# Fixed places for the fourth and fifth norm in a hybrid encoder block: sums and row spreads between value and query products, and the second quarter's query and key products pass by pass

## The chip, the cores and the metric

The kernel runs on one core of one Trainium2 chip. The metric is device time in microseconds of a whole execution, as the median of several executions: 1527.71 us before the change (three runs, 1527.10 to 1528.05). Beside it stands one execution recorded by the hardware profiler, which names every instruction of every engine with its start and its length. PE is the matrix engine (TensorE), DVE the vector engine (VectorE), ACT the scalar engine (ScalarE), POOL is GpSimd, and SP (SyncE) issues most of the data transfers (DMAs).

## The reference, cut to what matters

One block of an encoder on 1024 frames and 16 learned meta tokens, 1024 features wide: a norm, a token mixer with four mLSTM heads and four retention heads, a second norm, and a gated MLP with a causal convolution.

```
def rmsnorm(x, g):
    y = xf * lax.rsqrt(jnp.mean(xf * xf, axis=-1, keepdims=True) + EPS)
    return (y * g)
...
    h = jnp.concatenate([meta, x], axis=1)
    h = h + token_mixer(rmsnorm(h, norm_mix_g[l]), w_in[l], ...)
    h = h + channel_mixer(rmsnorm(h, norm_ffn_g[l]), ...)
    return rmsnorm(h, norm_final_g)[:, N_META:]
```

Inside the token mixer `proj = up @ w_in` gives queries, keys, values and gates of all heads. The change lies at the very beginning: the first norm, and the first products of its result with the weights of head 4.

## The kernel before, in words

**Layout.** Features lie on the 128 partitions and positions on the free axis. Each product of 32-bit numbers is made of three products of a rounded type: high part times high part, high times low, low times high. So every operand is split in two: ACT copies it to the rounded type (the high part), and DVE subtracts that from the original (the low part). The normed stream is held in four blocks named after the half of the positions and the half of the features: "11" and "12" (first half of the positions), "21" and "22" (second half). `UB[...]` holds high and low part, `u21h` and `u21l` in the profile. Later, sums and differences of the blocks (S1 to S4) are made too, for a Winograd-like scheme with seven products in place of eight; `usum` and `usplit` make them.

**The five norms.** The 1040 positions are normed in five ranges (`RNG`): 144, 128 and 256 positions of the first half, 272 and 256 of the second. Counted from one, the fourth norm is `r = 3` and the fifth `r = 4`. One norm has these steps:

- `norm_sums` (L850): ACT squares both feature halves (L855, L863), DVE adds them (L867) and halves the sum again (L870, remembered as `last["added"]`); PE then sums over the partitions (L826, "pca"), ACT takes the root (L828) and DVE the reciprocal (L829, "rcola"). With `late=True` the part from the PE sums on is returned as a function, to be called later.
- `norm_rows`: PE spreads the reciprocal over the partitions (L838, "pra").
- `norm_split` (L882): DVE scales with the gain and the spread factor, eight instructions (L890); ACT casts each feature half to the high part (L891); DVE subtracts the low parts (L895, `last["pace"]`).

**The products around them.** `v4_group(c, ...)` makes values and gate inputs of head 4 for one chunk of 128 positions, with the stream as the stationary operand: three passes (high-high, high-low, low-high) of eight matmuls each (L954). ACT evacuates the values (L957) and DVE the gate inputs (L958). `q4_group(i, half, j0, j1, ...)` makes queries (i = 0) or keys (i = 1) of head 4 for one quarter of the positions, 24 matmuls, the three products of one feature block right behind each other (L901 to L903), and an evacuation by ACT (L966, "rawq", "rawk"). `q4_pair` makes queries and keys of the first quarter together and pass by pass: high-high for both, then high-low, then low-high (L979), with the third norm's sums ahead of the first pass and its row spread ahead of the second.

**What sets the order.** Up to the products of the output gate of head 4 ("o" products, po4x and po4y, L911 to L913), nothing is fixed but data dependencies and the pairs that `after(later, first)` adds: the framework's scheduler simulates the engines' time and takes, for each engine, what it holds to be ready, earlier written work first. So matmuls that are written later fill places that it thinks would stand empty: in the profile of before, query products stand between those of a value group. From the o products on (`pinned[0] = True`) PE, DVE and ACT follow program order, which a planner inside the kernel has dealt out with costs of its own. Transfers are not pinned. Each engine's queue is then executed in order.

**The stretch of the change** (L1782 to L1850): norm 1, value group 1 with norm 2, groups 0 and 2, the pair of the first quarter with norm 3, norm 4's sums, groups 3 and 4, norm 4's split, norm 5's sums, queries and keys of the second quarter, norm 5's split, the sums of blocks for S1 and S2, groups 5 and 6, queries and keys of the third quarter, groups 7 and 8, queries and keys of the last quarter, the split of S3, two copies of block "12" into other buffers (x12, L1845), and the split of S4. The products go round a ring of PSUM banks (pa, pb, sA, num). The buffers of S3 are those of block 21's parts, those of S1 are the raw blocks 11 and 22; the rotation tables (`tables_load`, "A<-rot_d" in the profile) are loaded into the buffers that S1's sums leave.

Of the kernel before, what the change touches and what calls it, by code (L numbers as in the profile page):

```python
# [36 lines left out]
SB = 528  # L37
# [52 lines left out]
def body(ctx, tc, h_in, vecs, cst, mask_in, rot, w_v0, w_vp, w_g, w_out, w_up, w_gate, w_down, out):  # L90
# [10 lines left out]
    def dep(later, first, sync):  # L101
        kind = mybir.DependencyClass.Sync if sync else mybir.DependencyClass.NoSync
        tc.add_manual_dep(later.ins, first.ins.name, mybir.DependencyInfo(kind, mybir.DependencyReason.DATA), reason="order")

    def after(later, first):
        dep(later, first, False)

    last = {}
    G, PE, V, AC = nc.gpsimd, nc.tensor, nc.vector, nc.scalar
# [114 lines left out]
    raws = [st.tile([P, T], F32, name=f"raw{x}") for x in "qk"]  # L224
# [60 lines left out]
    def pp(name, tag):  # L285
        return ps.tile([P, 512], F32, tag=tag, name=name, bufs=PSB[tag])
# [94 lines left out]
    def spawn(g, q=pend, key=None):  # L381
        if dealt[0]:
            if next(g, pend) is not pend:
                q.append(g)
                until[id(g)] = fin[0]
                owner[id(g)] = key
        else:
            for _ in g:
                pass
# [262 lines left out]
    sums = {(g, st_, k): dram.tile([P, 2 * HB], F32, name=f"ws{g}{st_}_{k}") for g, n in (("w", 8), ("d", KD)) for st_ in ("65", "73") for k in range(n)}  # L652
# [166 lines left out]
    def rms_sums(ss, t0, t1, nm, col, tag, more=()):  # L819
        n = t1 - t0  # L820
        o = n % P
        subs = ([(0, P, o)] if o else []) + [(i, P, P) for i in range(o, n, P)]
        pc = rps("pc" + nm, tag)
        for i, (o, w, _) in enumerate(subs):
            for a in (ss, *more):
                last["sums"] = PE.matmul(pc[:w, i:i + 1], a[:, o:o + w], cs[:, C_M01 + P - 1:C_M01 + P], start=a is ss, stop=a is (ss, *more)[-1])  # L826
        ns = len(subs)
        last["sqrt"] = AC.activation(col[:, :ns], pc[:, :ns], AF.Sqrt, bias=epsc, scale=1.0 / D)  # L828
        last["recip"] = V.reciprocal(col[:, :ns], col[:, :ns])  # L829
        return n, subs, pc, col, nm  # L830
# [19 lines left out]
    def norm_sums(r, late=False):  # L850
        half, j0, j1 = RNG[r]
        n = j1 - j0
        xs = [xf[f"{half + 1}{i + 1}"][:, :, j0:j1] for i in (0, 1)]
        sq = [x[:, :, j0:j1] for x in sqs]
        m = AC.activation(sq[0], xs[0], AF.Square)  # L855
        if r:
            after(m, last["sqrt"])
        if r < 2:
            m = V.tensor_tensor(sq[1], xs[1], xs[1], ALU.mult)
            if r:  # L860
                after(m, last["scale"])
        else:
            after(AC.activation(sq[1], xs[1], AF.Square), last["sqrt"])  # L863
        if r == 1:
            ss = [x[:, k] for x in sq for k in range(4)]
        else:
            m = V.tensor_tensor(sq[0], sq[0], sq[1], ALU.add)  # L867
            if r:
                after(m, last["pace"] if r in (2, 3) else last["recip"])
            last["added"] = V.tensor_tensor(sq[0][:, 0:2], sq[0][:, 0:2], sq[0][:, 2:4], ALU.add)  # L870
            ss = [sq[0][:, k] for k in range(2)]

        def sums():
            norms[r] = xs, rms_sums(ss[0], 0, n, f"a{r}", tmp.tile([P, 5], F32, tag="rcol", name=f"rcola{r}"), "tr", ss[1:])
        if late:
            return sums
        sums()

    def norm_rows(r):
        norms[r] += (rms_rows(norms[r][1], None, "upd"),)  # L880

    def norm_split(r):  # L882
        half, j0, j1 = RNG[r]
        if len(norms[r]) < 3:
            norm_rows(r)
        xs, got, pr = norms.pop(r)
        parts_ = [[u[:, :, j0:j1] for u in UB[f"{half + 1}{i + 1}"]] for i in range(2)]
        for i, x in enumerate(xs):
            for k in range(4):
                last["scale"] = V.scalar_tensor_tensor(x[:, k], x[:, k], vec[:, V_MIX + 4 * i + k:V_MIX + 4 * i + k + 1], pr, ALU.mult, ALU.mult)  # L890
            m = last["cast"] = AC.copy(parts_[i][0], x)  # L891
            if r == 0:
                last["first"] = m
        for x, (h_, l_) in zip(xs, parts_):
            last["pace"] = V.tensor_tensor(l_, x, h_.bitcast(F32), ALU.subtract)  # L895
        if r == 0:
            for i, x in enumerate(xs):
                V.tensor_copy(ug[:, 4 * i:4 * i + 4], x[:, :, :32])
# [31 lines left out]

    vtile[4] = [vslot(0, "v4lo"), vslot(1, "v4hi")]

    def v4_group(c, tag, between=None):
        t0, L = CH[c]
        nv = 264
        pv = pp(f"pv4_{c}", tag)
        if c == 0:
            for i in range(2):
                for j in range(4):
                    after(PE.matmul(pv[32 * j:32 * j + 32, :nv], ug[:, 4 * i + j, :], w0raw[i][:, j * nv:(j + 1) * nv],  # L940
                                    start=i == 0, stop=i == 1, tile_position=(0, 32 * j)), last["rows"])
            t = vz[:META, 264:264 + nv]
            spawn(quads(t, pv, nv))
            V.tensor_copy(gts[:META, :, 0, :], t[:, DV:].rearrange("p (a b) -> p a b", a=2))
            return
        half = c > 4
        j0 = t0 - 512 * half
        for i, j in ((0, 0), (0, 1), (1, 0)):
            if i and between:
                between()  # L950
            for kb in range(KB):
                u = UB[f"{half + 1}{kb // 4 + 1}"][i]
                o = kb % 4 * nv
                m = PE.matmul(pv[:, :nv], u[:, kb % 4, j0:j0 + L], (w0hi, w0lo)[j][kb // 4][:, o:o + nv], start=i + j + kb == 0, stop=i == 1 and kb == KB - 1, skip_group_check=True)  # L954
                if i and between:
                    after(m, last["rows"])
        AC.copy(vtile[4][half][:, (c - 1) % 4 * VW:(c - 1) % 4 * VW + DV], pv[:, :DV])  # L957
        V.tensor_copy(gts[:, :, c, :], pv[:, DV:nv].rearrange("p (a b) -> p a b", a=2))  # L958

    def q4_group(i, half, j0, j1, tag):  # L960
        w = need(("q4", i), 1 - i)
        pt = pp(f"pq4{i}{half}{j0}", tag)[:, :j1 - j0]
        for kb in range(KB):
            u = UB[f"{half + 1}{kb // 4 + 1}"]
            mm3(pt, tuple(x[:, kb % 4 * P:(kb % 4 + 1) * P] for x in w[kb // 4]), tuple(x[:, kb % 4, j0:j1] for x in u), kb == 0, kb == KB - 1)
        AC.copy(raws[i][:, half * 512 + j0:half * 512 + j1], pt)  # L966

    def q4_pair(half, j0, j1, tags, between):
        w = [need(("q4", i), 1 - i) for i in range(2)]
        pt = [pp(f"pq4{i}{half}{j0}", tags[i])[:, :j1 - j0] for i in range(2)]  # L970
        for p, (a, b) in enumerate(((0, 0), (0, 1), (1, 0))):
            if p == 0:
                between()
            if p == 1:
                norm_rows(2)
            for i in range(2):
                for kb in range(KB):
                    u = UB[f"{half + 1}{kb // 4 + 1}"][b]
                    m = PE.matmul(pt[i], w[i][kb // 4][a][:, kb % 4 * P:(kb % 4 + 1) * P], u[:, kb % 4, j0:j1], start=p + kb == 0, stop=p == 2 and kb == KB - 1, skip_group_check=True)  # L979
                    after(m, last["rows" if p else "sums"])  # L980
        AC.copy(raws[0][:, half * 512 + j0:half * 512 + j1], pt[0])
        yield
        after(AC.copy(raws[1][:, half * 512 + j0:half * 512 + j1], pt[1]), last["cast"])

    ROWS = [("x", "11"), ("y", "12"), ("x", "S2"), ("y", "S1"), ("x", "S3"), ("y", "S4"), ("x", "22")]
# [794 lines left out]
    ring0 = tag_ring()  # L1780
# [10 lines left out]
    v4_group(2, next(ring0))  # L1791
    third = norm_sums(2, True)
    need(("q4", 0), 1)
    pair = q4_pair(0, 0, 272, [next(ring0), next(ring0)], third)
    next(pair)
    norm_split(2)
    next(pair, None)
    norm_sums(3)
    for c in (3, 4):
        v4_group(c, next(ring0))  # L1800
    norm_split(3)
    norm_sums(4)
    for i in range(2):
        q4_group(i, 0, 272, SB, next(ring0))
    norm_split(4)

    s1 = [st.tile([P, 2 * SB], F32, tag=f"A{i + 1}", name=f"s1_{i}").rearrange("p (k j) -> p k j", k=2) for i in range(2)]
# [1 line left out]
    def part(x, i):  # L1809
        return s1[i] if x == "S1" else xf[x][:, 2 * i:2 * i + 2]  # L1810
# [19 lines left out]
    usum(1, "11", "12", "12")  # L1830
    usplit("S1", "S1", "uh3", "ul3")
    need(("o", 4, 1), 0)
    for c in (5, 6):
        v4_group(c, next(ring0))
    for i in range(2):
        q4_group(i, 1, 16, 272, next(ring0))
    for c in (7, 8):
# [4 lines left out]
    x12 = [vslot(2 + i, f"s4_{i}").rearrange("p (k j) -> p k j", k=2) for i in range(2)]  # L1842
    tables_load(4)
    for i in range(2):
        AC.copy(x12[i], part("12", i))  # L1845
    s1[:] = x12
    need(("o", 4, 1))
    usplit("S4", "S1", "uh2", "ul2")
# [719 lines left out]
```

## Time and profile before

| | us |
|---|---|
| median of three runs | 1527.71 (1527.10 to 1528.05) |
| the profiled execution | 1526.2 |
| its span, first to last instruction | 1524.4 |
| PE busy in the span | 1486.6 |
| DVE busy | 1090.0 |
| ACT busy | 756.4 |
| POOL busy | 72.1 |
| mean granted PE clock | 0.996 of full |

A line of the profile in order of time reads: start, length, engine, line of the kernel, operation, output<-inputs, tile shape, types, how many instructions are merged, and in brackets the idle time before them with what ended it. Times are microseconds from the first instruction. A matmul's length is that of its passage through a pipeline, so products that follow each other start every 0.12 us though each is shown with 0.28. In the list of waits the three numbers are the total, how often, and the longest.

### The profile page before, as it was taken

The page shows a single profiled execution, that of the slowest core. Times are in us where ns is not written, and L with a number is a line of the kernel's source. Part 1 is how long each engine was busy: PE and PEld are TensorE (multiplying, and loading weights), DVE is VectorE, ACT ScalarE, POOL GpSimd, SP SyncE. Part 2 cuts the span into 40 slices and gives each one's busy share as a digit, 9 for nine tenths or more (in the row PEclk, how much of TensorE's full clock was granted, in tenths as well). Part 3 has the DMA queues.
Part 4 walks back from the last instruction along what each step waited for, and adds up shares of the span by engine and source line. Part 5 has one row for each costly group of instructions (what it writes and reads, how often), then busy time and mean ns, then how long its engine had stood idle before and what let it go on. Part 6 is the DMA issues. An engine that isn't in the chain of part 4 may idle for free.

```text
span 1524.4 us, 25487 instructions
## 1 busy us (share of the span) xinstructions
PE 1486.6 (98%) x9929; PEld 1348.3 (88%) x9929; DVE 1090.0 (72%) x2087; ACT 756.4 (50%) x1455; POOL 72.1 (5%) x157
## 2 busy tenths in 40 slices
PE   7989999999999999999999999999999999999997
PEld 7888999999999999987888998999999999888887
DVE  6785868678777677846867787767666666778667
ACT  4465655554655455554454565444444444344443
POOL 1000000000000000000000001222220000000000
PEclk9999999999999999999999999999999999999999
DMA  6022255323533355697333248887772224933313
GB/s 232 2 87 60 84 161 195 110 78 118 186 120 98 125 166 185 198 394 262 110 114 132 80 128 239 199 210 191 178 196 78 83 81 157 370 105 109 97 42 111
DMA packets 104586, 223.81 MB, mean 147 GB/s; under 512 B 10520, under 2 KB 33760, under 8 KB 104288
## 3 DMA queue, kind: packets, MB, share of 16 engines
q1 hardware_dynamic: 89824, 191.68, 37.8%
q0 software_dynamic: 8448, 23.07, 7.6%
q10 hardware_dynamic: 6192, 7.41, 1.4%
q8 instruction: 78, 1.28, 0.3%
q14 instruction: 44, 0.36, 0.1%
HBM read 178.05 MB, written 67.15 MB: 161 GB/s over the span
## 4 chain that ended last, share of the span: by engine, by line
PE 88%; DVE 7%; DMA 3%; ACT 1%; issue 1%; DVEq 0%; SPq 0%; ACTq 0%
PE pdx L913 3%; PE pdx L912 3%; PE pdx L911 3%; PE pup_x L912 2%; PE pga_x L911 2%; PE pup_x L913 2%; PE pup_x L911 2%; PE pga_x L912 2%; PE pga_x L913 2%; PE pdy L913 2%; PE pdy L912 2%; PE pdy L911 2%; PE n L1603 2%; PE pwx L913 2%; PE u L1601 2%; PE pwx L911 2%
## 5 line engine op out<-in xcount | busy, mean ns | idle before, releaser
L782 ACT CAST hi_up<-raw_up 128x512 fp32r<-128x512 f32 (+1 forms) x52 | 36.4, 719 | 107.7 <-PE pga_z L912 61.1
L783 DVE TENSOR_TENSOR lo_up<-raw_up,hi_up 128x512 fp32r<-128x512 f32 (+1 forms) x52 | 41.3, 810 | 38.2 <-ACT hi_up L782 37.5
L783 DVE TENSOR_TENSOR lo_ga<-fraw_ga,hi_ga 128x512 fp32r<-128x512 f32 (+1 forms) x52 | 41.9, 809 | 37.1 <-ACT hi_ga L782 36.9
L911 PE MATMUL pup_x<-uh_g,hi_up 128*128 128x256 f32 (+1 forms) x240 | 67.2, 283 | 1.2 <-ACT uh_g L1965 1.2
L912 PE MATMUL pup_x<-ul_g,hi_up 128*128 128x256 f32 (+1 forms) x240 | 67.4, 282 | 0.1
L913 PE MATMUL pup_x<-uh_g,lo_up 128*128 128x256 f32 (+1 forms) x240 | 66.4, 282 | 0.0
L783 DVE TENSOR_TENSOR lo_d<-rd,hi_d 128x1024 fp32r<-128x1024 f32 (+1 forms) x34 | 37.7, 1114 | 32.8 <-ACT hi_d L782 32.7
L782 ACT CAST hi_ga<-fraw_ga 128x512 fp32r<-128x512 f32 (+1 forms) x52 | 36.4, 719 | 45.4 <-PE pup_z L912 21.9
L913 PE MATMUL pdx<-uh_d,lo_d 128*128 128x512 f32 (+1 forms) x156 | 57.9, 375 | 0.0
L912 PE MATMUL pdx<-ul_d,hi_d 128*128 128x512 f32 (+1 forms) x156 | 57.8, 374 | 0.0
L782 ACT CAST hi_d<-rd 128x1024 fp32r<-128x1024 f32 (+1 forms) x34 | 32.3, 959 | 49.2 <-PE pdy L912 32.5
L913 PE MATMUL pdy<-uh_d,lo_d 128*128 128x512 f32 x132 | 51.9, 393 | 0.0
L912 PE MATMUL pdy<-ul_d,hi_d 128*128 128x512 f32 x132 | 51.7, 392 | 0.0
L911 PE MATMUL pdx<-uh_d,hi_d 128*128 128x512 f32 (+1 forms) x156 | 48.5, 372 | 0.0
L911 PE MATMUL pdy<-uh_d,hi_d 128*128 128x512 f32 x132 | 47.9, 389 | 0.0
L911 PE MATMUL pga_x<-uh_g,hi_ga 128*128 128x512 f32 x120 | 47.5, 396 | 0.0
L912 PE MATMUL pga_x<-ul_g,hi_ga 128*128 128x512 f32 x120 | 47.5, 396 | 0.0
L911 PEld LDWEIGHTS pup_x<-uh_g,hi_up 128*128 128x128 f32 x240 | 45.3, 189 | 2.3 <-ACT uh_g L1965 1.4
L913 PE MATMUL pga_x<-uh_g,lo_ga 128*128 128x512 f32 x120 | 47.1, 393 | 0.0
L912 PEld LDWEIGHTS pup_x<-ul_g,hi_up 128*128 128x128 f32 x240 | 45.4, 189 | 1.0 <-DVE ul_g L1966 0.3
L913 PEld LDWEIGHTS pup_x<-uh_g,lo_up 128*128 128x128 f32 x240 | 44.8, 189 | 0.8
L1670 DVE SCALAR_TENSOR_TENSOR mx<-tr,vec,sig 128x386 f32<-128x386 f32 (+2 forms) x42 | 24.0, 571 | 21.5 <-PE tr L1662 16.0
(1698 smaller groups left out, 5738.8 us busy)
## 6 DMA issues: line engine op xcount, KB each, us to landing
raw_up<-w_up_d SPq DMA_DIRECT2D x22, 512.0 KB, 6.4
fraw_ga<-w_gate_d SPq DMA_DIRECT2D x22, 512.0 KB, 5.0
acts<-cv SPq DMA_DIRECT2D x44, 256.0 KB, 4.2
wsd<-w_down_d POOLq DMA_DIRECT2D x44, 256.0 KB, 7.0
rd<-wsd SPq DMA_DIRECT2D x22, 512.0 KB, 3.6
raw_w<-w_out_d SPq DMA_DIRECT2D x20, 512.0 KB, 6.8
wsw<-raw_w SPq DMA_DIRECT2D x32, 256.0 KB, 3.2
raw_m<-w_out_d SPq DMA_DIRECT2D x14, 512.0 KB, 4.0
```

The lines of the kernel that those rows point to most:

```text
L782: AC.copy(hi[:, o:o + n], x)
L783: V.tensor_tensor(lo[:, o:o + n], x, hi[:, o:o + n].bitcast(F32), ALU.subtract)
L911: m.append(PE.matmul(pt, ah, xh_, start=first and k == 0, stop=False, skip_group_check=True))
L912: PE.matmul(pt, ah, xl_, start=False, stop=False, skip_group_check=True)
L913: m.append(PE.matmul(pt, al, xh_, start=False, stop=last and k == n - 1, skip_group_check=True))
L1601: PE.matmul(up[:, :nv], kw[:L], v, start=True, stop=True)
L1603: PE.matmul(pn[:L, :nv], pt[:L, :L], v, start=True, stop=c == 0)
L1670: return V.scalar_tensor_tensor(dst, tr[:, x0 - t0:x1 - t0], vec[:, g:g + 1], sig(b, p)[:, x0 - a0:x1 - a0], ALU.mult, ALU.mult)
```

## The change

- Norm 4's sums on PE are called inside a `q4_pair` for the second quarter, which takes the place of its two `q4_group` calls; its row spread comes between the queries' and the keys' high-high products. Queries of that pass are ordered after the sums, all later products of the pair after the rows. Both evacuations of this pair are ordered after the last cast of norm 4.
- `norm_split` is divided into `norm_scale` (scaling and casts) and `norm_lows` (low parts). Between the two of norm 4 stand norm 5's squares and their sum on DVE, ordered after norm 4's scaling (before: after the last reciprocal); norm 4's low parts are ordered after that sum.
- Value groups 5 and 6 move ahead of norm 5's split. Norm 5's sums on PE stand ahead of group 5's low-high pass, and its row spread ahead of group 6's high-low pass, with the products around them ordered after them.
- The two x12 copies are ordered after the last raw copy (`last["raw"]`).

```diff
             if r:
-                after(m, last["pace"] if r in (2, 3) else last["recip"])
+                after(m, last["pace"] if r in (2, 3) else last["scale"] if r == 4 else last["recip"])
...
+    def norm_split(r):
+        norm_scale(r)
+        norm_lows(r)
+
+    def norm_scale(r):
...
+    def norm_lows(r):
+        xs, parts_ = scaled.pop(r)
         for x, (h_, l_) in zip(xs, parts_):
             last["pace"] = V.tensor_tensor(l_, x, h_.bitcast(F32), ALU.subtract)
+            if r == 3:
+                after(last["pace"], last["added"])
...
-    def v4_group(c, tag, between=None):
+    def v4_group(c, tag, between=None, at=1):
...
         for i, j in ((0, 0), (0, 1), (1, 0)):
-            if i and between:
+            hooked = between and (i or j > at - 1 and not at)
+            if between and (i, j) == ((1, 0) if at else (0, 1)):
                 between()
...
-                if i and between:
+                if hooked:
                     after(m, last["rows"])
...
-        AC.copy(raws[i][:, half * 512 + j0:half * 512 + j1], pt)
+        last["raw"] = AC.copy(raws[i][:, half * 512 + j0:half * 512 + j1], pt)
...
-            if p == 1:
-                norm_rows(2)
+            if p == 1 and r == 2:
+                norm_rows(r)
             for i in range(2):
+                if r == 3 and p == 0 and i:
+                    norm_rows(r)
...
-                    after(m, last["rows" if p else "sums"])
-        AC.copy(raws[0][:, half * 512 + j0:half * 512 + j1], pt[0])
+                    after(m, last["rows" if p or r == 3 and i else "sums"])
+        if r == 2:
+            AC.copy(raws[0][:, half * 512 + j0:half * 512 + j1], pt[0])
         yield
+        if r == 3:
+            after(AC.copy(raws[0][:, half * 512 + j0:half * 512 + j1], pt[0]), last["cast"])
         after(AC.copy(raws[1][:, half * 512 + j0:half * 512 + j1], pt[1]), last["cast"])
...
-    norm_sums(3)
+    fourth = norm_sums(3, True)
     for c in (3, 4):
         v4_group(c, next(ring0))
-    norm_split(3)
-    norm_sums(4)
-    for i in range(2):
-        q4_group(i, 0, 272, SB, next(ring0))
+    pair = q4_pair(0, 272, SB, [next(ring0), next(ring0)], 3, fourth)
+    next(pair)
+    norm_scale(3)
+    fifth = norm_sums(4, True)
+    norm_lows(3)
+    next(pair, None)
+
+    def fifth_sums():
+        fifth()
+        last["rows"] = last["sums"]
+    v4_group(5, next(ring0), fifth_sums)
+    v4_group(6, next(ring0), lambda: norm_rows(4), 0)
     norm_split(4)
...
-    for c in (5, 6):
-        v4_group(c, next(ring0))
...
     for i in range(2):
-        AC.copy(x12[i], part("12", i))
+        after(AC.copy(x12[i], part("12", i)), last["raw"])
```

More of the change, by code (lines that the diff above doesn't have):

```diff
@@ L880, in norm_rows @@
         norms[r] += (rms_rows(norms[r][1], None, "upd"),)
+    scaled = {}
     def norm_split(r):
+        norm_scale(r)
+        norm_lows(r)
+    def norm_scale(r):
         half, j0, j1 = RNG[r]
@@ L887, in norm_split @@
         parts_ = [[u[:, :, j0:j1] for u in UB[f"{half + 1}{i + 1}"]] for i in range(2)]
+        scaled[r] = xs, parts_
         for i, x in enumerate(xs):
@@ L965, in q4_group, with q4_pair @@
             mm3(pt, tuple(x[:, kb % 4 * P:(kb % 4 + 1) * P] for x in w[kb // 4]), tuple(x[:, kb % 4, j0:j1] for x in u), kb == 0, kb == KB - 1)
-        AC.copy(raws[i][:, half * 512 + j0:half * 512 + j1], pt)
-    def q4_pair(half, j0, j1, tags, between):
+        last["raw"] = AC.copy(raws[i][:, half * 512 + j0:half * 512 + j1], pt)
+    def q4_pair(half, j0, j1, tags, r, between):
         w = [need(("q4", i), 1 - i) for i in range(2)]
@@ L1793, in body @@
     need(("q4", 0), 1)
-    pair = q4_pair(0, 0, 272, [next(ring0), next(ring0)], third)
+    pair = q4_pair(0, 0, 272, [next(ring0), next(ring0)], 2, third)
     next(pair)
```

## The prediction

> **What bounds the kernel now.** I read the page first, then busy time by stretch, then each engine in order of time, then the chain of work that ended last.
>
> ```profile
> span 1524.4 us, 25487 instructions
> PE 1486.6 (98%) x9929; PEld 1348.3 (88%) x9929; DVE 1090.0 (72%) x2087; ACT 756.4 (50%) x1455; POOL 72.1 (5%) x157
> ```
>
> TensorE (PE) carries the kernel, and a change in order can only win where PE stands still. Busy time by stretch (first the length, then busy us and count for PE, PEld, DVE, ACT, POOL, then granted clock, DMA share, GB/s):
>
> ```profile
> 33.00:46.70 13.70, 13.70 (x116) 13.50 (x114) 7.91 (x13) 4.46 (x9) 0.00 (x0) 1.00 0.01 2
> 46.70:73.00 26.30, 24.77 (x209) 24.77 (x209) 23.83 (x37) 10.89 (x18) 0.00 (x0) 1.00 0.01 2
> 73.00:93.00 20.00, 15.73 (x138) 14.57 (x136) 17.46 (x28) 15.96 (x27) 0.00 (x0) 1.00 0.48 159
> 93.00:126.00 33.00, 29.29 (x213) 27.25 (x214) 22.36 (x66) 15.34 (x33) 0.33 (x3) 0.95 0.26 66
> 126.00:160.00 34.00, 34.00 (x256) 32.62 (x254) 22.83 (x56) 20.59 (x40) 0.11 (x1) 1.00 0.07 24
> ```
>
> PE is idle 1.53 us before 73, 4.27 us from 73 to 93, 3.71 us from 93 to 126, and not at all for the next 34 us. So what the edited stretch (33 to 73) wins must pass the two loose stretches behind it; from 126 on PE is the bound and keeps what arrives. PE in order of time:
>
> ```profile
> 39.08 0.28 PE L902 MATMUL pq<-u11l,hi_q 128*128 128x256 f32 x1
> ...
> 40.29 1.39 PE L826 MATMUL pca<-cs,sqr 128*128 128x1 f32 x12
> ...
> 44.46 0.83 PE L838 MATMUL pra<-cs,rcola 128*128 128x16 f32 x6
> ...
> 48.23 1.24 PE L954 MATMUL pv<-w0hiq,u21h 128*128 128x264 f32 x8 [1.53 <-ACT u21h L891]
> ...
> 49.54 0.95 PE L826 MATMUL pca<-cs,sqr 128*128 128x1 f32 x8
> ...
> 56.21 0.61 PE L838 MATMUL pra<-cs,rcola 128*128 128x128 f32 x4
> ...
> 71.08 0.28 PE L903 MATMUL pq<-u21h,lo_q 128*128 128x256 f32 x1
> ...
> 72.62 0.28 PE L911 MATMUL po4x<-u11h,hi_o 128*128 128x258 f32 x1
> ...
> 76.18 0.39 PE L911 MATMUL po4x<-u11h,hi_o 128*128 128x256 f32 x1 [1.95 <-ACT rawk L966]
> ...
> 90.36 0.28 PE L913 MATMUL po4x<-uS3h,lo_o 128*128 128x256 f32 x1
> 92.95 0.39 PE L911 MATMUL po4y<-uS4h,hi_o 128*128 128x258 f32 x1 [2.31 <-ACT sig L1003]
> ```
>
> The fourth norm's sums end at 41.68 (40.29 + 1.39); its row spread (L838) comes 2.8 us later, behind query and key products that the scheduler put first. So u21h is late and PE runs out at 46.70. VectorE (DVE) over the same time:
>
> ```profile
> 37.11 0.73 DVE L870 TENSOR_TENSOR sqr<-sqr 128x544 f32<-128x544 f32 x1
> ...
> 42.01 0.18 DVE L829 RECIPROCAL rcola<-rcola 128x3 f32<-128x3 f32 x1 [2.16 <-ACT rcola L828]
> 43.91 1.22 DVE L867 TENSOR_TENSOR sqr<-sqr,sqr 128x1024 f32<-128x1024 f32 x1 [1.71 <-ACT sqr L863]
> 45.32 3.36 DVE L890 SCALAR_TENSOR_TENSOR x<-x,vec,pra 128x272 f32<-128x272 f32 x8 [0.19 <-PE pra L838]
> 48.59 0.69 DVE L870 TENSOR_TENSOR sqr<-sqr 128x512 f32<-128x512 f32 x1
> 49.20 1.29 DVE L479 TENSOR_TENSOR lo_o<-raw_o4a,hi_o 128x512 fp32r<-128x512 f32 x2
> 50.40 1.29 DVE L895 TENSOR_TENSOR u21l<-x,u21h 128x1088 fp32r<-128x1088 f32 x1
> 51.60 1.29 DVE L895 TENSOR_TENSOR u22l<-x,u22h 128x1088 fp32r<-128x1088 f32 x1
> 52.80 0.69 DVE L568 TENSOR_TENSOR raw_o4a<-raw_o4a,raw_o4b 128x512 f32<-128x512 f32 x1
> 53.40 0.17 DVE L829 RECIPROCAL rcola<-rcola 128x2 f32<-128x2 f32 x1
> ...
> 56.85 3.22 DVE L890 SCALAR_TENSOR_TENSOR x<-x,vec,pra 128x256 f32<-128x256 f32 x8
> ...
> 85.45 0.71 DVE L1213 TENSOR_TENSOR qT<-rawq,A 128x528 f32<-128x528 f32 x1
> 86.73 0.71 DVE L1214 TENSOR_TENSOR kT<-kT,A 128x528 f32<-128x528 f32 x1 [0.57 <-DMA A<-rot_d]
> ```
>
> Reciprocal done at 42.19, scaling (L890) begun at 45.32. The fifth: reciprocal done at 53.57, spread at 56.21, scaling at 56.85. From 56.85 to the rotation at 85.45 DVE has no marked wait, and that queue leads to the gates, whose ScalarE (ACT) work delays the evacuation that PE awaits at 92.95. So a late norm is paid for twice: PE's 1.53 us at once, and some 40 us later through DVE and ACT.
>
> **The change part by part.** No arithmetic is added: the same matmuls, casts and DVE operations, no DMA issue more or less; what is queued on SP and POOL keeps its program order. All costs are waits.
>
> *Value groups 3 and 4, then the fourth sums.* Ten query products (39.08 to 40.29, 0.12 us each) and two earlier ones that had filled a hole near 34 now stand behind the sums. The hole reopens: +0.25 (between 0 and 0.5; the two products took 0.24). The sums start at 40.29 - 1.44 + 0.25 = 39.1; their input is there at 37.84 (37.11 + 0.73), so no wait. They end at 40.5. Root and reciprocal took 0.51 (41.68 to 42.19) and lie under the first query pass, 8 x 0.12 = 0.96. Rows begin at 41.4, take 0.83, scaling begins at 42.3 instead of 45.32: 3.0 earlier.
>
> *Queries and keys pass by pass.* Of 48 products 40 are left after the rows: 41.4 + 0.58 + 40 x 0.12 = 46.8. The casts need half a scaling (1.64) and one cast of 1.1 each: first half 45.0, second 46.7. Value group 5 finds its data, and the 1.53 us stall goes. Both evacuations of the pair wait for the last cast; nothing takes their banks before group 7, so I cost that at nothing, under groups 5 and 6.
>
> *The fifth sum ahead of the fourth's lows.* DVE in start-to-start times: scaling 3.27, add 1.15, half-add 0.61, lows 2.40, the o-weight work (L479 twice, L568 and its equal in size L571) 1.2 + 0.6 + 0.6, reciprocal 0.13: 9.96 in all, done at 52.3. Sums input at 47.3, lows at 49.7. PE: group 5's high passes end at 48.7, sums (0.81) at 49.5, its low pass at 50.5, group 6's first pass at 51.5, rows (0.61) at 52.1. What waits behind the pins is group 6's 16 products; query products of the second half carry no pin and can fill. Fifth scaling at 52.2: 4.6 earlier; should the scheduler fill with query products first, 3.0, the fourth's lead. I take 4.1, nearer the row sum.
>
> *x12 after the last raw copy.* ACT from 68 to 84:
>
> ```profile
> 68.31 0.86 ACT L957 COPY v4hi<-pv 128x256 f32<-128x256 f32 x2 [6.62 <-PE pv L954]
> ...
> 71.80 2.06 ACT L1823 CAST uS3h<-x 128x1056 fp32r<-128x1056 f32 x2
> 73.75 1.07 ACT L1845 COPY s<-x 128x1056 f32<-128x1056 f32 x1
> ...
> 75.76 0.37 ACT L966 COPY rawk<-pq 128x256 f32<-128x256 f32 x1
> ...
> 82.61 0.63 ACT L1210 COPY kT<-rawq 64x528 f32<-64x528 f32 x1
> ```
>
> ACT has no gap from 68.31 to 82.61. The key products end by 72.8, behind which the first o product (72.62) is already running, yet their copy (rawk, L966) stands behind uS3h, one x12 copy (L1845) and two weight casts, and PE waits 1.95 for it. With x12 barred from going ahead, 0.97 goes; I take 1.5 of the 1.95, since PE also arrives when uS3h is nearly through (between 0 and 1.95). Queued behind the two x12 copies is only the S4 split, which PE needs at the sixth of seven steps, at 92.95.
>
> The Trainium skill (TensorE: Matmul & The Clock Gate, section on architectural detail) says ACT and DVE are strict FIFO: a barred copy bars all behind it. The trace agrees, rawk standing 3 us behind its product; by that rule alone the pin gives back up to 1.94 (two copies) and the sum would be 1.6 us.
>
> *The sum.* PE at 76: -1.53 + 0.25 - 1.5 = -2.8. DVE at 56.85: -4.1. Of ACT's 14.3 us before 82.61 the value copies, uS2h (two casts like uS3h's) and the first raw copy (0.75 + 2.0 + 0.26 = 3.0) move ahead; 11.3 are left, and uS3h cannot start before PE's last use of u21 (71.36, now 70.1). ACT is through at 81.4, 1.2 earlier; the last weight's low part follows on DVE in 0.6, so the rotation starts near 82.0: 3.4 earlier, or 3.9 at 86.73 if the table is no longer waited for (0.57). PE reaches 90.64 - 2.8 = 87.8 and is released at 92.95 - 3.5 = 89.4, so the later lead counts: **3.5 us**. Behind 92.95 the order is fixed by the program on PE, DVE and ACT, and PE's other waits
>
> ```profile
> PE pe L1272 <- DVE gates L1265: 1.5, 1, 1.5
> PE s L1556 <- DVE pt L1580: 1.4, 1, 1.4
> ```
>
> stay as they are and shift along. Span 1524.4 - 3.5 = 1520.9; the profiled run took 1.8 us more than its span (1526.2), and the median of the runs, 1527.71, is 1.5 above that run: 1524.2. Ends: a gain of 1.2 (ACT alone leads) to 5.1 (4.6 + 0.5).
>
> **The rivals.** *Hidden by ACT.* DVE's lead ends in a queue that ACT feeds; the casts of S3, S1, x12 and S4 all come after 70, and if x12 or the weight casts go ahead of uS1h, uS1l and the table load behind it come late. Against it: ACT marks no idle time before 83.89, so 3.0 us of its work can truly move. Gain 1.2: 1526.5.
>
> *Slower, by the SP queue.* PE, DVE and ACT are pinned to program order from the o products on, DMA issue is not. The chain that ended last passes a load and its issue:
>
> ```profile
> 113.85 9.94 DMA raw_vp<-w_vp_d
> ```
>
> If the moved start lets another load pass this one, or a table load stand behind it, the value weights land up to one such time later. It decides from 3.5 us on; at a full 9.9 the kernel is 6.4 slower: 1534.1; at half, 1529.2. For it: PE goes idle soon after it lands (the 1.4 above). Against it: its issue waits for a DVE step that moves along.
>
> *Clock.* Behind PE's idle time at 99 to 101 the clock is halved:
>
> ```profile
> 102.00:104.00 2.00, 2.00 (x12) 2.00 (x11) 1.97 (x4) 0.00 (x0) 0.00 (x0) 0.50 0.00 0
> ```
>
> The 0.95 from 93 to 126 is 33 x 0.05 = 1.65 us. If the waits fall otherwise this goes: 3.5 + 1.6 = 5.1, 1522.6; a new long wait could bring another. The Trainium skill (same page, What's actually happening) has the clock halve after an idle window of some 3.4 us that runs free of the kernel; the trace agrees with the halving, not with a whole idle window, since PE still had work in it.
>
> **How the numbers follow.** Forecast 0.50, hidden by ACT 0.23, slower by SP 0.19, clock 0.08. No change is what lies within 0.2% (3.06 us), about what a measurement of this kernel can tell. The forecast's own range, 1522.6 to 1526.0, crosses that line: three quarters of it, and the clock case, are faster: 0.46. Hidden, the rest, and a few small delays give 0.39; the larger delays 0.15. The range 1521.4 to 1530.2 leaves out larger delays (0.13) and a clock gain on top of the best lead (0.05).
>
> **What would show it.** Right: fourth scaling near 42.3 and fifth near 52.2; no PE wait at the first product of u21h; rawk ahead of L1845 and the wait at po4x under 0.6; rotation near 82. Wrong: a PE wait at group 5 or 6 for L829 or L870 over 1 us, L1213 later than 84, a changed order of the loads at 79 to 114, or a halved clock before 90.

## The result, and the profile after

The changed kernel takes 1530.96 us (median of 20 runs, 1528.66 to 1535.14), the kernel before 1528.05 us (20 runs beside them, 1526.69 to 1531.86). The ratio is 1.0017, with a 95% interval of 1.0010 to 1.0024: 0.1 to 0.24% slower. That is inside the 0.2% within which the prediction spoke of no change, but the whole interval lies above a ratio of 1; the forecast of 3.5 us faster is refuted, and the time lies just above the range (1530.2). The profiled execution of after took 1529.4 us, and its span is 3.2 us longer than that of before (1527.6 against 1524.4).

The busy time of after in the stretches shown of before:

```profile
33.00:46.70 13.70, 13.70 (x117) 13.69 (x117) 9.64 (x18) 6.43 (x10) 0.00 (x0) 1.00 0.01 2
46.70:73.00 26.30, 25.92 (x217) 25.72 (x215) 24.08 (x34) 9.53 (x17) 0.00 (x0) 1.00 0.01 2
73.00:93.00 20.00, 14.76 (x126) 13.61 (x126) 14.05 (x21) 14.65 (x24) 0.00 (x0) 1.00 0.46 159
93.00:126.00 33.00, 28.98 (x210) 26.95 (x210) 22.92 (x67) 15.41 (x34) 0.32 (x3) 0.95 0.27 66
```

Up to 73 the change does what it is for: PE's idle time there falls from 1.53 to 0.38 us. From 73 to 93 it rises from 4.27 to 5.24 us, and DVE, which had 17.46 us of work in that stretch, now has 14.05: some 2.0 us of that work has moved ahead of 73 (33.72 us of it from 33 to 73, before 31.74), and for the rest DVE stands and waits. PE of after in order of time:

```profile
41.24 0.83 PE L838 MATMUL pra<-cs,rcola 128*128 128x16 f32 x6
...
46.61 0.66 PE L967 MATMUL pv<-w0hiq,u21h 128*128 128x264 f32 x4
...
53.91 0.28 PE L914 MATMUL pq<-u22l,hi_q 128*128 128x256 f32 x1
54.03 0.61 PE L838 MATMUL pra<-cs,rcola 128*128 128x128 f32 x4
...
74.58 0.39 PE L923 MATMUL po4x<-u11h,hi_o 128*128 128x256 f32 x1 [1.96 <-ACT rawk L979]
...
94.41 0.39 PE L923 MATMUL po4y<-uS4h,hi_o 128*128 128x258 f32 x1 [4.57 <-ACT sig L1021]
```

The fourth norm's rows (41.24) stand inside the query products, where they were put, and u21h's first product (46.61) waits for nothing. PE then reaches the last o products (po4y) sooner and waits there twice as long, 4.57 us instead of 2.31, so that it leaves them 1.46 us later than before (94.41, 92.95). DVE of after shows where that comes from:

```profile
42.11 3.36 DVE L897 SCALAR_TENSOR_TENSOR x<-x,vec,pra 128x272 f32<-128x272 f32 x8 [1.25 <-PE pra L838]
...
50.85 0.16 DVE L829 RECIPROCAL rcola<-rcola 128x2 f32<-128x2 f32 x1
...
54.67 3.22 DVE L897 SCALAR_TENSOR_TENSOR x<-x,vec,pra 128x256 f32<-128x256 f32 x8 [0.72 <-PE pra L838]
...
78.14 2.42 DVE L1850 TENSOR_TENSOR uS1l<-s,uS1h 128x1056 fp32r<-128x1056 f32 x2
...
85.28 0.71 DVE L1231 TENSOR_TENSOR qT<-rawq,A 128x528 f32<-128x528 f32 x1 [0.84 <-DMA A<-rot_d]
88.20 0.71 DVE L1232 TENSOR_TENSOR kT<-kT,A 128x528 f32<-128x528 f32 x1 [2.21 <-DMA A<-rot_d]
...
90.94 0.13 DVE L1262 TENSOR_SCALAR gsm<-vec 36x1 f32<-36x1 f32 x1
```

The lead over before is 3.2 us at the fourth scaling (42.11, 45.32), 2.2 at the fifth (54.67, 56.85), 0.2 at the first step of the rotation (85.28, 85.45), and at the second step it has become a loss of 1.5 (88.20, 86.73). Both steps now wait for their tables (A from rot_d). The gates' first DVE step (gsm) follows at once, and by it the ACT work that releases PE at 94.41. Two queues stand behind this. ACT of after:

```profile
74.17 0.36 ACT L979 COPY rawk<-pq 128x256 f32<-128x256 f32 x1
74.43 2.05 ACT L1869 COPY s<-x 128x1056 f32<-128x1056 f32 x2
...
76.65 2.05 ACT L1849 CAST uS1h<-s 128x1056 fp32r<-128x1056 f32 x2
```

Both x12 copies (L1869) now stand between rawk and the casts of S1; before, one of them went ahead of rawk (73.75). Next, the loads that SP issues, first before, then after:

```profile
80.33 0.33 SPq L1135 DMA_DIRECT2D A<-rot_d  x1
81.49 0.33 SPq L1136 DMA_DIRECT2D A<-rot_d  x1
81.92 0.86 SPq L328 DMA_DIRECT2D raw_vp<-w_vp_d  x2
```

```profile
79.75 0.33 SPq L328 DMA_DIRECT2D raw_vp<-w_vp_d  x1
80.18 0.37 SPq L1153 DMA_DIRECT2D A<-rot_d  x1
80.64 0.38 SPq L328 DMA_DIRECT2D raw_vp<-w_vp_d  x1
81.12 0.39 SPq L1154 DMA_DIRECT2D A<-rot_d  x1
```

The order has changed: two loads of value weights (raw_vp), which no engine is seen to wait for from 73 to 93, stand among the table loads. The list of SP's waits says what it costs:

```profile
SPq L1135 <- DVE uS1l L1824: 0.8, 1, 0.8
```

```profile
SPq L328 <- PE pvm L722: 2.5, 1, 2.5
```

Before (the upper line), the first table load left SP as soon as the first half of uS1l was done, and the second at its second half. After, SP waits 2.5 us for a product that frees the buffer of a value weight, with the first table load behind it. Not all of that is lost, since uS1l itself starts only at 78.14: with the distances of before, 1.42 us from its start to the first table load (80.33 - 78.91) and 2.58 to the second (81.49 - 78.91), the loads could have left at 79.56 and 80.72, an estimate, and left at 80.18 and 81.12. The larger part is the landing: the second table is used 7.1 us after its issue (81.12 to 88.20) instead of 5.2 (81.49 to 86.73), with 512 KB of value weights issued ahead of each table.

From 93 to 126 PE makes up its lateness and loses it again; the mean clock is 0.95 in both. PE is 1.46 us late at po4y. Further on it comes to a product of scores (s) at 124.2 in both kernels, and waits there, first before, then after:

```profile
125.65 0.49 PE L1556 MATMUL s<-qT,kT 128*128 128x128 f32 x2 [1.43 <-DVE pt L1580]
```

```profile
126.67 0.49 PE L1574 MATMUL s<-qT,kT 128*128 128x128 f32 x2 [2.47 <-DVE pt L1598]
```

The DVE step named there stands behind ACT's casts of a value weight (hi_vp), which wait for its load (raw_vp) and start at 123.81 before, 124.83 after. SP issues that load 1.93 us behind the first that brings back the stored gates (A from scr), in both kernels: 111.92 and 113.85 before, 112.95 and 114.88 after. So what carries the loss past 93 is the chain from the gates to this load, 1.03 us late, and not PE.

The two recorded executions stay 1.0 us apart up to 230. The rest of the 3.2 us of span comes in two steps. From 390 to 410 PE of after stands still for 1.16 us and PE of before not at all; and near 713 the clock is halved in both, in after for longer: it is 0.50 from 713 to 715 and 0.65 from 715 to 717 in before, 0.50 from 713 to 719 in after. What made these two isn't shown.

### The profile page after: what moved, and what is told of

Same layout as the page of the kernel before. It is cut to its first block, busy times and chain, and to the rows that moved or that the text cites. A ratio compares the mean times of both kernels' runs of the same rounds, so it can differ in the third digit from the quotient of the medians.

```text
span 1527.6 us, 25490 instructions
## 1 busy us (share of the span) xinstructions
PE 1488.0 (97%) x9929; PEld 1349.2 (88%) x9929; DVE 1089.4 (71%) x2087; ACT 756.4 (50%) x1455; POOL 72.2 (5%) x157
## 4 chain that ended last, share of the span: by engine, by line
PE 88%; DVE 6%; DMA 3%; ACT 2%; issue 1%; SPq 0%; ACTq 0%; DVEq 0%
PE pdx L925 3%; PE pdx L924 3%; PE pdx L923 3%; PE pup_x L924 2%; PE pup_x L925 2%; PE pga_x L923 2%; PE pup_x L923 2%; PE pga_x L924 2%; PE pga_x L925 2%; PE pdy L925 2%; PE pdy L924 2%; PE pdy L923 2%; PE n L1621 2%; PE pwx L925 2%; PE u L1619 2%; PE pwx L923 2%
```

## The experiments

Two theories. *The prologue's theory*: the fixed places themselves buy nothing, because PE and DVE only wait elsewhere. *The queue theory*: the fixed places are worth about what was forecast, and the ordering edge on the x12 copies, a single `after` of this change, gives it away through ACT's order and SP's. Ratios are to the kernel before, run beside on the same chip. Every one of these kernels computes the whole output.

### The edge taken away, and the edge alone

```diff
 # e2: after, without the edge (e3: before, with it)
-        after(AC.copy(x12[i], part("12", i)), last["raw"])
+        AC.copy(x12[i], part("12", i))
```

> The changed kernel without the order edge that puts the x12 copies after the last raw copy; the norms stay in their fixed places. The scheduler then puts the x12 copies before the S3 casts and the tables ahead of the value weights again. Theory 1 with rival A: the S1 casts start near 74.5 instead of 76.65, the tables are issued 2 us earlier than before the change, the second rotation step comes at 84 to 85, and the kernel is 1.5 to 2.5 us faster than before (ratio 0.9985). Rival C: slower than before or the same, since the norms are where they were.

> The kernel before, with only the order edge of the x12 copies added; the norms are as before. The scheduler then puts both loads of value weights ahead of the rotation tables. Theory 1: the second rotation step comes 1.5 to 3 us later than 86.7 and the kernel is 1 to 3 us slower than before. Rival A alone: S1 casts 1 us later, at most 1 us slower. Rival C: no difference to before.

Without the edge: 1525.83 us, ratio 0.9981 (0.9972 to 0.9989). The edge alone on the kernel before: 1533.12 us, 1.0026 (1.0015 to 1.0037). One `after` decides the sign of the whole change: without it the change wins 0.19%, 2.9 us, not far from the 3.5 forecast, and the edge costs 0.36% on top of that (1.0017 over 0.9981). On the kernel before it costs 4.0 us, more than the 1 to 3 expected. DVE without the edge:

```profile
42.34 3.36 DVE L897 SCALAR_TENSOR_TENSOR x<-x,vec,pra 128x272 f32<-128x272 f32 x8 [1.25 <-PE pra L838]
...
84.48 0.70 DVE L1231 TENSOR_TENSOR qT<-rawq,A 128x528 f32<-128x528 f32 x1
85.58 0.71 DVE L1232 TENSOR_TENSOR kT<-kT,A 128x528 f32<-128x528 f32 x1 [0.40 <-DMA A<-rot_d]
...
88.32 0.13 DVE L1262 TENSOR_SCALAR gsm<-vec 36x1 f32<-36x1 f32 x1
```

The second step of the rotation is 1.15 us ahead of before, 2.62 ahead of after. On ACT both x12 copies lie ahead of the casts of S3:

```profile
70.47 1.07 ACT L1869 COPY s<-x 128x1056 f32<-128x1056 f32 x1
...
71.70 1.08 ACT L1869 COPY s<-x 128x1056 f32<-128x1056 f32 x1
72.68 2.04 ACT L1849 CAST uS3h<-x 128x1056 fp32r<-128x1056 f32 x2
```

SP, without the edge and then with the edge alone:

```profile
79.34 0.33 SPq L1153 DMA_DIRECT2D A<-rot_d  x1
80.50 0.33 SPq L1154 DMA_DIRECT2D A<-rot_d  x1
82.74 0.80 SPq L328 DMA_DIRECT2D raw_vp<-w_vp_d  x2
```

```profile
83.44 0.80 SPq L328 DMA_DIRECT2D raw_vp<-w_vp_d  x2
84.33 0.38 SPq L1135 DMA_DIRECT2D A<-rot_d  x1
84.81 0.38 SPq L1136 DMA_DIRECT2D A<-rot_d  x1
```

So an edge between ACT copies turns round the order of loads on SP, in both kernels. With the edge alone the tables are used 8.1 and 9.0 us after their issue (84.33 to 92.44, 84.81 to 93.78), behind two value weights. The other times of that execution, 1535.67 us and the slowest of its eight, are not compared here: the granted clock is 0.50 in it from 50 to 56, where before has 1.00. The likely link, argued and not shown, is that the scheduler orders SP by its own simulated times, in which a later S1 makes the tables ready later. The edge has two effects at once, which the next three kernels take apart.

### The order on ACT and the order on SP, each alone and both

```diff
 # SP: tables first (e1, e4)
-            nc.sync.dma_start(x[:, o:o + y.shape[1]], y)
+            m = nc.sync.dma_start(x[:, o:o + y.shape[1]], y)
+            if nm.startswith("vp0_2"):
+                after(m, last["rot"])
...
-            nc.sync.dma_start(A2, rot[:, 1])
+            last["rot"] = nc.sync.dma_start(A2, rot[:, 1])
 # ACT: casts of S1 ahead of x12, the edge to the raw copy kept (e4, e9)
-            AC.copy(h_, part(x, i))
+            last[nm] = AC.copy(h_, part(x, i))
...
-        after(AC.copy(x12[i], part("12", i)), last["raw"])
+        m = AC.copy(x12[i], part("12", i))
+        after(m, last["raw"])
+        after(m, last["S1"])
```

> The changed kernel, with the two loads of value weights (raw_vp 21 and 22) ordered behind the rotation tables on the SP queue, as they stood before the change. Theory 1 (the tables come late because value weights went ahead of them): the second rotation step, which stood at 88.2 us in the changed kernel and at 86.7 before, comes at 85 to 86; the wait of PE for the sig evacuation falls from 4.6 to under 2.5 us; the time falls by 1 to 2.7 us against the changed kernel, to about that of before. Rival A (the S1 casts stand too late on ACT behind the x12 copies): the tables cannot be issued earlier than 79 to 80.5, so at most the time of before, no gain over it. Rival C (the fixed places of the norms cost the time): no difference to the changed kernel, 0.17% slower than before.

> The changed kernel with the tables ahead of the value weights, and the x12 copies ordered after the S1 casts too. Theory 1 and rival A together: the S1 casts start near 74.5, the tables are issued by 78.5, the second rotation step comes at 84 to 85 where DVE itself is through, and the kernel is 1.5 to 2.5 us faster than before, 1 us or more faster than with the tables alone put first. If rival A plays no part: the same as with the tables alone put first.

> The S1 casts ahead of the x12 copies as in the kernel at 0.9975, but the loads of value weights left where the changed kernel has them, ahead of the rotation tables on SP. The fourth corner of S1 early or late by tables first or second. If the place on SP costs by itself: the tables are held until the slot of the first value weights is free (near 79.7), the second rotation step comes at 87.5 to 88.2, and the time is that of the changed kernel, 1.0005 to 1.0020. If the S1 casts alone carry the gain: 0.9975 to 0.9985.

| ratio to before (95%) | value weights first on SP | tables first on SP |
|---|---|---|
| x12 ahead of S1 on ACT | 1.0017 (1.0010 to 1.0024), after | 1.0002 (0.9993 to 1.0011), e1 |
| S1 ahead of x12 on ACT | 1.0011 (1.0003 to 1.0020), e9 | 0.9975 (0.9966 to 0.9984), e4 |

The order on ACT alone buys nothing that can be told, the order on SP alone 0.15% (its interval and that of after just overlap), both together 0.42%. The profiles say why they don't add up. With S1 early and the weights still first (e9):

```profile
76.41 2.42 DVE L1850 TENSOR_TENSOR uS1l<-s,uS1h 128x1056 fp32r<-128x1056 f32 x2
...
85.22 0.71 DVE L1231 TENSOR_TENSOR qT<-rawq,A 128x528 f32<-128x528 f32 x1 [2.02 <-DMA A<-rot_d]
88.11 0.71 DVE L1232 TENSOR_TENSOR kT<-kT,A 128x528 f32<-128x528 f32 x1 [2.19 <-DMA A<-rot_d]
```

uS1l is 1.73 us earlier than in after, and the rotation starts at the same time: SP again waits 2.5 us for pvm ahead of the tables. With the tables first and S1 late (e1) it is the other way round:

```profile
SPq L1155 <- DVE uS1l L1852: 3.7, 1, 3.7
```

SP stands 3.7 us before the first table load, for uS1l, and the second step of the rotation comes at 87.58, not at the 85 to 86 that was expected. Only with both (e4) is neither late:

```profile
42.93 3.36 DVE L899 SCALAR_TENSOR_TENSOR x<-x,vec,pra 128x272 f32<-128x272 f32 x8 [1.25 <-PE pra L840]
...
85.43 0.70 DVE L1233 TENSOR_TENSOR qT<-rawq,A 128x528 f32<-128x528 f32 x1
86.05 0.70 DVE L1234 TENSOR_TENSOR kT<-kT,A 128x528 f32<-128x528 f32 x1
...
88.79 0.13 DVE L1264 TENSOR_SCALAR gsm<-vec 36x1 f32<-36x1 f32 x1
```

```profile
75.53 2.05 ACT L1851 CAST uS1h<-s 128x1056 fp32r<-128x1056 f32 x2
```

No wait for a table is left, and counted from the fourth scaling the casts of S1 (the last fence, from ACT) start 32.60 us on (75.53 - 42.93) instead of 34.54 in after (76.65 - 42.11). This kernel, 1525.25 us, has the lowest ratio of all and beats before and after; it isn't told apart from the one without the edge (0.9981). In both the second step of the rotation was expected at 84 to 85 and came later, at 85.58 and 86.05; the times are better than the gain of 1.5 to 2.5 us that was expected with it.

### Half of the places

```diff
 # e5: after, with the fifth norm as before, and without the edge
-    norm_scale(3)
-    fifth = norm_sums(4, True)
-    norm_lows(3)
+    norm_split(3)
...
+    for c in (5, 6):
+        v4_group(c, next(ring0))
 # e6: after, with the fourth norm and the pair as before, and without the edge
-    fourth = norm_sums(3, True)
+    norm_sums(3)
-    pair = q4_pair(0, 272, SB, [next(ring0), next(ring0)], 3, fourth)
...
+    for i in range(2):
+        q4_group(i, 0, 272, SB, next(ring0))
```

> The norm places of the fourth norm alone: its sums and rows inside the pass-by-pass pair of the second quarter; the fifth norm, value groups 5 and 6 and the x12 copies stand as before the change. If the places of the norms are what gains: the 1.53 us wait of PE at the first product of u21h is gone, the fifth scaling comes 1.5 to 3 us earlier, and the kernel is 1 to 2 us faster than before (ratio 0.9990). If the gain of the kernel without the x12 edge (0.9981) comes from the ACT order alone: no difference to before.

> The places of the fifth norm alone: its squares and sum on DVE between the fourth's scaling and its lows, its sums and rows inside value groups 5 and 6; the fourth norm and the second quarter's products as before, no x12 edge. If the places of the norms gain: the 1.53 us wait at u21h stays, the fifth scaling comes 1 to 2 us earlier than 56.85, and the kernel is 0.5 to 1.5 us faster than before (ratio 0.9993). If the two parts gain only together: no difference to before.

The fourth alone: 1527.27 us, 0.9993 (0.9984 to 1.0002); the fifth alone: 1530.14 us, 1.0011 (1.0002 to 1.0021). Neither half gains anything that can be told, where both together reach 0.9981. With the fourth alone its scaling starts at 42.40 but the fifth's at 56.31, for which DVE waits 1.75 us: it is 0.54 us ahead of before, not 1.5 to 3, and the lead is lost one norm later.

With the fifth alone PE still waits 1.5 us for u21h, and 0.6 for u22h beside it. The fifth scaling comes at 60.36, 3.5 us later than before, where 1 to 2 us earlier was expected. But behind that wait the clock is halved in this execution from 50 to 56:

```profile
50.00:52.00 2.00, 2.00 (x11) 2.00 (x11) 2.00 (x3) 0.00 (x0) 0.00 (x0) 0.50 0.00 0
```

Before has the same wait and keeps 1.00. The eleven executions of this kernel have a mean clock of 0.9932, those of before beside them 0.9945. So neither half alone was seen to bring the gain; that the places of the fifth norm lose time by themselves isn't shown, since the clock may be most of that loss.

### PE's wait for the key copy

```diff
 # e10: e2 with tables first, and the later o-weight casts behind the key copy
+                if key[:2] == ("o", 4) and key[2] > 2:
+                    after(m, last["raw"])
 # e11: the same, and the casts of S3 too.  e7: as e11, but on e4
+            if nm == "S3":
+                after(m, last["raw"])
```

> The changed kernel without the x12 edge (0.9981), the later o-weight casts ordered behind the key copy and the tables kept first; the order of the S1 and S4 casts stays as there. PE's wait at po4x falls from 3.2 to about 2.1. If that wait is hidden by the later ones: the same time, 0.9976 to 0.9986. If it counts in full: 0.9974.

> As the last one, with the S3 casts behind the key copy too, S1 and S4 casts still in the same order behind them. PE's wait at po4x falls under 0.6. If it counts: 0.9962 to 0.9970. If it is hidden: the po4y wait opens by 1 to 2 us instead, and the time is that of the kernel without the edge (0.9976 to 0.9986) or later by what the S3 casts lose, up to 0.5 us.

> As the kernel with the S1 casts ahead of x12 and the tables first (ratio 0.9975), and the S3 casts and the later o-weight casts ordered after the key copy, so that PE finds its bank free at the second o product. If the 1.96 us wait of PE at po4x is worth its length: it falls under 0.5 us and the kernel is another 1.5 us faster (0.9965). If it is hidden, because PE waits for the gates' chain at po4y anyway: po4x falls, po4y rises by as much, and the time is the same as 0.9975 within its interval.

PE waits for rawk 3.2 us without the edge, 2.2 in e10, 0.3 in e11 and e7. No time is won by it: 1527.15 us, 0.9989 (0.9980 to 0.9998); 1527.36 us, 0.9995 (0.9986 to 1.0004); 1530.73 us, 1.0010 (1.0001 to 1.0018), against 0.9981, 0.9981 and 0.9975 without these edges. e7 is clearly slower than e4; the intervals of e10 and e11 overlap with that of e2. In e11 the wait comes back further on, for ACT's sig: 1.3 us at po4x (87.81) and 3.4 at po4y (92.84).

This wait of PE is not what leads. The times go rather with the time at which the gates begin on DVE (gsm), from which the chain to the value weight at 113.85 runs. For every kernel with the fourth norm in its new place, from the start of its scaling to gsm in the profiled execution:

| kernel | scaling to gsm, us | ratio |
|---|---|---|
| e4, S1 and tables first | 45.86 | 0.9975 |
| e2, no edge | 45.98 | 0.9981 |
| e5, fourth alone, no edge | 46.77 | 0.9993 |
| e11, key copy first | 47.04 | 0.9995 |
| e10, key copy earlier | 47.76 | 0.9989 |
| e7, key copy first, on e4 | 48.39 | 1.0010 |
| e1, tables first | 48.44 | 1.0002 |
| after | 48.83 | 1.0017 |
| e9, S1 first | 49.08 | 1.0011 |

The order of the two columns is nearly the same, though the first is of one execution of each kernel. Some 3 us in this stretch go with some 6 us of time (0.42%). Why each counts about double is only in part known. In the recorded executions e2 is 1.16 us ahead of before from 126 to 230 and after 1.03 behind: 2.2 apart, where the medians differ by 5.1. A part is the clock: its mean over the runs is 0.9936 in after, 0.9943 in e2 and 0.9950 in e4. In the 32 runs of before beside e2 and e4, 0.001 less of it goes with 1.06 us more, so after would lose some 0.7 us to e2 and 1.5 to e4 by it (an estimate). The rest stays open.

### The good queue orders without the places

> The kernel before, norms untouched, with the x12 copies ordered after the S1 casts and the value weights after the tables. If the norms' places are worth about 3 us when ACT and SP let them through: this is 2 to 4 us slower than the same orders on the changed kernel (0.9975), so 0.9990 to 1.0005 of before. If the ACT and SP orders were all of that gain: 0.9975 here too.

The edit is that of e4, on the kernel before: 1531.48 us, 1.0019 (1.0011 to 1.0028), slower than the 0.9990 to 1.0005 expected, though e4 gains by the same edges. ACT there:

```profile
82.37 0.63 ACT L1213 COPY kT<-rawq 64x528 f32<-64x528 f32 x1
83.02 1.08 ACT L1825 CAST uS4h<-s 128x1056 fp32r<-128x1056 f32 x1
```

One cast of S4 has fallen behind the rotation's copies, so DVE's half of uS4l comes between the two steps of the rotation, and PE's wait at po4y grows to 4.0 us (e7 shows the same order, both S4 casts behind the copies, and 4.9). So the edges of e4 gain nothing without the norms' places, and 0.9975 there is not theirs alone. But the same edges didn't give the same order on ACT here, and whether that cast alone makes the loss wasn't tried: what e4's exact order would be worth on the kernel before stays open.

## Why the prediction was wrong

- **Fourth norm: right.** Scaling near 42.3 was forecast, 42.11 measured; the 1.53 us wait is gone; the hole of 0.25 did not open (PE is busy 13.70 of 13.70 us before 46.70).
- **Fifth norm: right in kind, half the size.** The step took a lead of 4.1 us, with 3.0 as its lower end; it is 2.2. The reciprocal came sooner than worked out (50.85), but its rows only at 54.03, behind the query products from 51.17 to 53.91. The step named them ("carry no pin and can fill") and priced that too low: even its lower end of 3.0 supposed such a fill.
- **The step that failed: x12 after the last raw copy.** "Queued behind the two x12 copies is only the S4 split." The casts of S1 are queued there too, although S1's split is written ahead of x12. The profile of before has them behind the second x12 copy already, in rows that the step left out of its list:

```profile
76.29 1.09 ACT L1845 COPY s<-x 128x1056 f32<-128x1056 f32 x1
77.26 2.06 ACT L1823 CAST uS1h<-s 128x1056 fp32r<-128x1056 f32 x2
```

With the edge the scheduler moved both copies from their place ahead of uS3h (70.47 and 71.70 without the edge) to the place right behind rawk, and left S1 behind them. Behind those casts are uS1l, the table loads that it releases, the rotation and the gates. The step priced what the edge lets forward (rawk) and not what it pushes back. Nor did it bring the 1.5 us of PE time: rawk is 1.6 us earlier (74.17, 75.76), but PE is too, and the wait stays at 1.96.
- **"No DMA issue more or less; what is queued on SP and POOL keeps its program order."** The first half holds, the second doesn't: the loads at 79.75 and 80.64 went ahead of tables. The rows of before quoted from ACT, DVE and PE had nothing from SP at this place; the one row of a load was at 113.85.
- **The sum.** Rotation near 82.0 and release of PE at 89.4 were forecast; 85.28 with 88.20, and 94.41, came. With the edge away the time is 2.9 us under before, inside the forecast's own bounds of 1.2 to 5.1, but not by its path, so the agreement is in part luck: the rotation is 0.97 us ahead of before there and the gates 1.15, where 3.4 was forecast. Even in e4, with no wait for a table, the rotation starts 42.50 us behind the fourth scaling (85.43 - 42.93), where the sum took 39.7 (82.0 - 42.3). One term of it: uS3h was to start at 70.1 and started at 71.18, because PE had taken eleven o products (61.69 to 62.89) ahead of its last query and key products. The step counted on ACT to set the rotation; in e2 and e4 DVE comes to it straight from work of its own. (A gain of 1.2 gives 1526.5, not the 1526.0 at which the part on the numbers ends the forecast's range; nothing here hangs on that.)
- **The rivals.** *Hidden by ACT* had the first link ("if x12 or the weight casts go ahead of uS1h, uS1l and the table load behind it come late") and ended it at a smaller gain. *Slower, by the SP queue* had the second ("a table load stand behind it"), with the price of a full landing at 113.85. The result is both, at 80; each was priced by itself, and the two together, which the 2 by 2 table shows to act together, had no chance of its own. The load at 113.85 did move too, by 1.03 us, as the gates that it follows did. *Clock* did not come in the stretch that it was priced in: 0.95 before and after.
- **The page's rule.** The Trainium skill (TensorE: Matmul & The Clock Gate, section on architectural detail) has ACT as a strict FIFO. The trace agrees, to the number: counted from the fourth scaling, the S1 casts come 1.94 us earlier where x12 stands behind them (34.54 against 32.60). What it would give back by that rule was there, and the sum of 1.6 that followed from it was nearer the truth than 3.5; that the tables behind those casts would lose their place on SP as well is not in the rule.

## What to carry to other kernels

Where a scheduler fills the queues, an ordering edge moves a barred instruction to a later place and pushes back whatever the scheduler leaves behind it there: list that work, on the instruction's own engine and, through the buffers that it frees, on the DMA queue. Follow the list to the next table or weight that somebody waits for, and price it beside the gain. Judge an edge of a composite change by itself as well, for here one line of it turned a gain of 0.19% into a loss of 0.17%.

## What the hardware showed that was not expected

**The same wait, with and without a halved clock.** PE waits 1.96 us for rawk in after and in e4. The stretch behind it (length, then busy us and count for PE, PEld, DVE, ACT, POOL, then granted clock, DMA share, GB/s), first after, then e4:

```profile
77.00:79.00 2.00, 2.00 (x18) 1.91 (x16) 1.20 (x2) 2.00 (x4) 0.00 (x0) 1.00 0.50 133
```

```profile
77.00:79.00 2.00, 2.00 (x11) 2.00 (x11) 2.00 (x4) 2.00 (x3) 0.00 (x0) 0.50 0.28 43
```

After keeps the full clock behind it, e4 halves it; the 4.57 us wait at po4y in after is followed by a clock of 0.50 from 95 to 97. The wait of 1.5 us at u21h is the same: in before the clock stays at 1.00 behind it, in the executions of e3 and e6 it is 0.50 from 50 to 56. So the same wait is followed by a halved clock in some executions and not in others, and the verdicts above go by medians. That e4's profiled execution, 1528.2 us, lies above its median isn't explained by this: its mean clock, 0.995, is that of most runs of e4.

**A load's landing time depends on what stands ahead of it.** The second table, 520 KB, took 5.2 us from issue to use in before and 5.1 without the edge (80.50 to 85.58). Ahead of it stood the first table and, 2.5 us earlier in both, a load of 512 KB (raw_q0a). In after, with two value weights of 512 KB each issued 1.37 and 0.48 us ahead of it, beside the first table, it took 7.1 us. e9, with the same loads ahead of it, shows 7.3 (80.79 to 88.11); e1, with none of these weights ahead, 5.6 (82.00 to 87.58).
